# Gate rows built in pairs of tokens, and the later fetched rows' dot products ordered behind the first pass, in a one-core hybrid decoder step

## The chip, the cores and the metric

The kernel runs on one core of a Trainium2 chip. The metric is the device time of one execution in microseconds (us). The kernel before took 1742.75 us, the median of 3 runs (1738.49 to 1743.54).

## The reference, cut to what matters

One decoder layer over 512 prompt tokens and 32 sample tokens of width 1024: retention and a convolution share an input and an output projection, then a layer norm, and then PEER, a retrieval of experts by product keys. PEER is where the change lies. For each token, 8 heads pick 16 of 16384 experts each; the output is the sum over the 128 picked experts of a gate times a GELU of a dot product times a row:

```
idx = e1 * N_KEYS + e2                                   # 128 x 128 experts
gate = jax.nn.softmax(sv.astype(jnp.float32), axis=-1)
u = jnp.take(peer_u, idx, axis=0)
act = jax.nn.gelu(jnp.einsum('phkd,pd->phk', u, xb), approximate=False)
vv = jnp.take(peer_v, idx, axis=0)
return jnp.einsum('phk,phkd->pd', gate * act, vv)
```

A last layer norm and the new states follow.

## The kernel before, in words

The tokens are treated in two ways. For 288 of them the kernel fetches the expert rows: the first 128 prompt tokens (index tile `I`), the 32 samples (`Is`) and 128 more prompt tokens (`Ib`). For the last 256 prompt tokens (ND = 256) it computes all 16384 experts densely and multiplies by a gate that is zero for experts not picked.

**Fetched rows.** `gather` (L561 to L578) is a generator; one step of it is one slot k. GpSimd issues an indirect DMA (L566) that brings 128 rows of 2048 float32 values, u and v side by side, into a tile `g`; VectorE multiplies the u half by x1 and sums it (L569, the dot); ScalarE takes the GELU and multiplies by the gate (L571, L572); VectorE adds the weighted v half to `acc` (L577). The pool `gp` holds three such tiles; a fourth, in `gx` or `gx2`, is used where k % 4 == 3 and the generator has 128 slots. The samples have 32 slots of four heads' groups side by side, so they have the three tiles of `gp` alone. `fetched` (L931) finishes the first tokens, then runs the samples and then the `Ib` tokens, each with a layer norm and an output at its end (`finish`, L580).

**Dense tokens.** The 128 first-key blocks e are in four groups, `EG` = (32, 20, 44, 32), kept as `Gb`, `Gc`, `Ga`, `Gd`. `scores_of(e)` (L770) loads 512 KB of u and runs 8 float32 matmuls into `sp` [128, 256] (each is two instructions in the profile). `v_stage(e)` (L901) loads 512 KB of v and runs 4 matmuls of 512 columns into `pB`. The loads go through SP's queue and share a pool of four tiles.

**The gates.** `build` (L843) makes the gates of 8 tokens (TB = 8) at a time. ScalarE writes `A` (L850: 8 instructions of 128 columns; L852: one of 1024), which is 1 at each token's first key and 0 elsewhere. VectorE writes `M` (L854), which marks the second key, and `B` (L857), which holds M times three bfloat16 parts of the gate. The layout of `M` is [key, token], 8 tokens beside each other, and that of `B` [part, key, token]. TensorE then multiplies, for each token, `A` by the token's column of `B` for the three parts (L863): the moving operand `B[:, q, :, t - t1]` reads one bfloat16 of every eight, that is, it goes on by 16 bytes per column. `first_keys` (L876, here called the first pass) does it for the first 96 second keys, 4 tokens to a PSUM tile, and multiplies the PSUM tile into `Gb`, `Ga` and `Gc` (L887, L889 for blocks of `Gc` that are not ready); every 12 tokens it also computes the scores of one block of `Gc` (`s_stage`, L867 to L874). `last_keys` (L894) does the last 32 keys, 16 tokens to a PSUM tile, for `Gd`.

**The order.** The first pass is emitted first; then `run` (L952) interleaves `phases` (v stages of all blocks, `last_keys`, and the scores of `Gd`) with two steps of `fetched` to each step of `phases`. The Tile framework schedules the instructions of each engine in its own modelled order of time, so instructions that are emitted later may stand earlier on an engine; each engine runs its list in order. `behind(ins, other)` (L163) puts an instruction after another of the same engine in that list, without a semaphore. After the last v stage, `layer_norm` from `pB` and four output DMAs end the kernel (L953 to L958).

Of the kernel before, what the change touches and what calls it, by code (L numbers as in the profile page):

```python
# [10 lines left out]
BF = mybir.dt.bfloat16  # L11
# [3 lines left out]
OP = mybir.AluOpType  # L15
# [3 lines left out]
D = 1024  # L19
# [5 lines left out]
PH, NK, TK = 8, 128, 16  # L25
# [6 lines left out]
TB = 8  # L32
KX = 60
UV = 4
EG = (32, 20, 44, 32)
E0S = (0, 32, 52, 96)

# [54 lines left out]
def tile_step(ctx: ExitStack, tc: tile.TileContext, a, o):  # L92
    nc = tc.nc
    V, S, T, G = nc.vector, nc.scalar, nc.tensor, nc.gpsimd

    per = ctx.enter_context(tc.tile_pool(name="per", bufs=1))
# [15 lines left out]
    def mmps():  # L112
        turn[0] += 1
        return banks[turn[0] % len(banks)].tile([128, 512], F32, name="mm")
# [7 lines left out]
    def cc(n):  # L122
        part, c, w = COFF[n]
        return cst[part][:, c:c + w]
# [29 lines left out]
    def bc_row(name, src, n, pool=per, q=nc.scalar, after=None):  # L154
        t = pool.tile([128, n], F32, name=name)
        load = q.dma_start(t, bass.AP(tensor=src.tensor, offset=src.offset, ap=[[0, 128], [1, n]]))
        if after is not None:
            behind(load, after)
        return t
# [3 lines left out]
    def behind(ins, other):  # L163
        tc.add_manual_dep(ins.ins, other.ins.name, mybir.DependencyInfo(
            mybir.DependencyClass.NoSync, mybir.DependencyReason.DATA), reason="order")

    def small(name, shape, dt=F32, bufs=2):
        return wk.tile(shape, dt, name=name, bufs=bufs)

    iot = per.tile([128, NK, TB], BF, name="iot")  # L170
    G.iota(iot, pattern=[[1, NK], [0, TB]], base=0, channel_multiplier=0, allow_small_or_imprecise_dtypes=True)
    row = per.tile([128, NK], BF, name="row")
    G.iota(row, pattern=[[1, NK]], base=0, channel_multiplier=0, allow_small_or_imprecise_dtypes=True)
    mhalf = per.tile([128, 1], F32, name="mhalf")
# [25 lines left out]
    def rope(w, blk, xT, n, col0, outs):  # L200

        def turn_head(h):
            pm = mmps()
            for c0, c1, dst in outs:
                A = dst[:, h]
                T.matmul(pm[:, c0:c1], perm, A, start=True, stop=True)
                B = small("ropeB", [128, 416], bufs=1)[:, :c1 - c0]
                V.tensor_mul(B, pm[:, c0:c1], cc("sin")[:, col0 + c0:col0 + c1])
                V.tensor_mul(A, A, cc("cos")[:, col0 + c0:col0 + c1])
                V.tensor_add(A, A, B)  # L210

# [251 lines left out]
    def mix_mm(n, gT, y, c0, wo, xT=None):  # L463

        banks_ = [mmps(), mmps()]
        if xT is not None:
            for q in range(2):
                residual(banks_[q], xT, range(q * 4, q * 4 + 4), c0)
        for src, k0 in ((y, 4), (gT, 0)):
            for q in range(2):  # L470
                for s in range(2):
                    for k in range(4):
                        last = T.matmul(banks_[q][:n, s * 256:(s + 1) * 256], src[:, k, c0:c0 + n],
                                        wo[q * 2 + s][:, k0 + k, :], start=(xT is None and k0 == 4 and s == 0 and k == 0),
                                        stop=(k0 == 0 and s == 1 and k == 3), skip_group_check=True)
        return banks_, last
# [79 lines left out]
        V.reciprocal(sm[:n], sm[:n])  # L556
        V.tensor_mul(gate[:n, e0:e0 + nh], ex[:n], sm[:n].unsqueeze(2).to_broadcast([n, nh, TK]))

    gx2 = []

    def gather(x1, idx, gate, acc, slots):  # L561

        for k in slots:
            spare = gx if x1 is x1_0 and k < KX else (gx2[0] if gx2 and len(slots) == 128 else None)
            t = (spare if spare is not None and k % 4 == 3 else gp).tile([128, 2 * D], F32, name="g")
            G.indirect_dma_start(out=t, out_offset=None, in_=a["uv"],  # L566
                                 in_offset=bass.IndirectOffsetOnAxis(ap=idx[:, k:k + 1], axis=0))
            act = gw.tile([128, 2], F32, name="act")
            V.scalar_tensor_tensor(t[:, :D], t[:, :D], 1.0, x1, op0=OP.mult, op1=OP.mult, accum_out=act[:, 0:1])  # L569
            wgt = gw.tile([128, 1], F32, name="wgt")  # L570
            S.activation(act[:, 1:2], act[:, 0:1], AF.Gelu)  # L571
            S.activation(wgt, act[:, 1:2], AF.Copy, scale=gate[:, k:k + 1])  # L572
            v = t[:, D:]
            if k == slots[0]:
                S.activation(acc, v, AF.Copy, scale=wgt)
            else:
                V.scalar_tensor_tensor(acc, v, wgt, acc, op0=OP.mult, op1=OP.add)  # L577
            yield  # L578
# [33 lines left out]
    e2T = per.tile([128, ND], BF, name="e2T")  # L612
    gtT = per.tile([128, 3, ND], BF, name="gtT")
# [37 lines left out]
    pm, last = mix_mm(128, g0, y0, 0, wo)  # L651
# [90 lines left out]
    mix_b(NS + 2 * C, C)  # L742
    caches()
    gather0 = gather(x1_0, I0, g0_gates, acc0, range(PH * TK))
    for _ in range(KX):
        next(gather0)
# [3 lines left out]

    uvp = ctx.enter_context(tc.tile_pool(name="uvp", bufs=UV, reuse_waits="tile"))
    gap = ctx.enter_context(tc.tile_pool(name="gap", bufs=1, reuse_waits="tile"))
# [9 lines left out]
    ln2 = [bc_row("lng", a["ln2_g"], D), bc_row("lnb", a["ln2_b"], D)]  # L762
    GW = {2: gap.tile([128, EG[2], ND], F32, name="Ga")}

    def place(e):

        g = max(i for i in range(4) if E0S[i] <= e)
        return GW[g][:, e - E0S[g]]

    def scores_of(e):  # L770

        u = uvp.tile([128, D], F32, name="uv").rearrange("p (k e) -> p k e", k=8)
        nc.sync.dma_start(u, a["ut"][e])
        sp = pdn.tile([128, ND], F32, name="sp")
        for k in range(8):
            T.matmul(sp, u[:, k], x1T[:, k, NG2:], start=(k == 0), stop=(k == 7))  # L776
        return sp
# [19 lines left out]
    for g in range(2):  # L797
# [9 lines left out]
        p = mmps().rearrange("p (q t) -> p q t", q=4)  # L807
# [16 lines left out]
    gb = gbs.enter_context(tc.tile_pool(name="gb", bufs=1, side="right", reuse_waits="tile"))  # L824
    GW[0] = gb.tile([128, EG[0], ND], F32, name="Gb")
    for e in range(EG[0]):
        S.activation(place(e), scores_of(e), AF.Gelu)
# [10 lines left out]
    for b in range(2):  # L838
        for q in range(2):
            residual(pB[b][q], x1T, range(q * 4, q * 4 + 4), NG2 + b * 128)  # L840
    GW[1] = gc.tile([128, EG[1], ND], F32, name="Gc")

    def build(bt, e0, ne, nt):  # L843


        pt = None
        for t1 in range(0, ND, TB):
            off = bt.tile([128, TB, NK], BF, name="off", bufs=1)
            for t in range(TB):
                S.activation(off[:, t], row, AF.Abs, bias=e1T[:, t1 + t:t1 + t + 1])  # L850
            A = bt.tile([128, TB, NK], BF, name="A")
            S.activation(A, off, AF.Relu, bias=1.0, scale=-1.0)  # L852
            M = bt.tile([128, ne, TB], BF, name="M")
            V.tensor_tensor(M, iot[:, e0:e0 + ne],  # L854
                            e2T[:, t1:t1 + TB].unsqueeze(1).to_broadcast([128, ne, TB]), op=OP.is_equal)
            B = bt.tile([128, 3, ne, TB], BF, name="B")
            V.tensor_tensor(B, M.unsqueeze(1).to_broadcast([128, 3, ne, TB]),  # L857
                            gtT[:, :, t1:t1 + TB].unsqueeze(2).to_broadcast([128, 3, ne, TB]), op=OP.mult)
            for t in range(t1, t1 + TB):
                if t % nt == 0:  # L860
                    pt = pdn.tile([128, nt, ne], F32, name="mm")
                for q in range(3):
                    T.matmul(pt[:, t % nt], A[:, t - t1], B[:, q, :, t - t1], start=(q == 0), stop=(q == 2))  # L863
                if t % nt == nt - 1:
                    yield pt, slice(t - nt + 1, t + 1)

# [9 lines left out]
    def first_keys():  # L876

        with tc.tile_pool(name="bt", bufs=2, reuse_waits="tile") as bt:
            done = 0
            for pt, ts in build(bt, 0, E0S[3], 4):  # L880
                for g, e0, e1, ready in ((0, 0, EG[0], True), (2, 0, EG[2], True), (1, 0, done, True), (1, done, EG[1], False)):
                    if e0 == e1:
                        continue
                    to = GW[g][:, e0:e1, ts]
                    part = pt[:, :, E0S[g] + e0:E0S[g] + e1].rearrange("p t e -> p e t")
                    if ready:
                        V.tensor_mul(to, to, part)  # L887
                    else:
                        V.tensor_copy(to, part)  # L889
                if ts.stop % 12 == 0 and done < EG[1]:  # L890
                    s_stage(E0S[1] + done, ts.stop)
                    done += 1

    def last_keys():  # L894

# [35 lines left out]
    def fetched():  # L931
# [3 lines left out]
        for g, c0, dst in (("s", 0, o[1].rearrange("b i d -> (b i) d")), ("b", NS, o[0][0, 128:256])):  # L935
# [11 lines left out]
            finish(x1g, [ac[:, 0:512], ac[:, 512:]], w_, [(0, w_, dst)], t)  # L947
            yield

    first_keys()  # L950
    gx2.append(ctx.enter_context(tc.tile_pool(name="gx2", bufs=1, reuse_waits="tile")))
    run((phases(), 1), (fetched(), 2))  # L952
    for b in range(2):  # L953
        t = uvp.tile([128, D], F32, name="uv")
# [50 lines left out]
```

## Time and profile before

| what | value |
|---|---|
| median of 3 runs | 1742.75 us |
| the profiled execution | 1744.1 us, span 1742.3 us |
| PE busy | 1635.5 us, 94% |
| VectorE (DVE) busy | 1250.1 us, 72% |
| ScalarE (ACT) busy | 603.4 us, 35% |
| GpSimd (POOL) busy | 375.6 us, 22% |
| moved by DMA | 503.75 MB, mean 289 GB/s |
| mean granted TensorE clock | 0.943 |

The profile is of one execution on the hardware. The span is the time from its first to its last instruction; 1.8 us of the execution lie outside it. PE is the matmul engine and PEld its weight loads, which run beside the matmuls; since matmuls are pipelined, a busy PE isn't a PE at its peak. Waits are put down to what released them. The chain of waits follows the work back from the last instruction and tells at each step what that step waited for.

### The profile page before, as it was taken

How to read it: one execution, taken by the hardware profiler on the slowest of the kernel's cores; microseconds unless marked ns; L12 is line 12 of the kernel's file. 1: busy time of each engine (PE TensorE's matmuls, PEld its weight loads, DVE VectorE, ACT ScalarE, POOL GpSimd, SP SyncE). 2: the span in 40 equal slices, each digit the busy share in tenths (PEclk: the TensorE clock that was granted, in tenths of full speed). 3: DMA queues.
4: the chain of work that ended last, by engine and by line, in shares of the span. 5: the costliest groups of instructions: out<-in, count | busy, mean ns of one | idle time of the engine just before them, and what ended most of it. 6: DMA issues, size and time to landing. Idle time of an engine off the chain costs nothing.

```text
span 1742.3 us, 20660 instructions
## 1 busy us (share of the span) xinstructions
PE 1635.5 (94%) x7014; PEld 1111.1 (64%) x7014; DVE 1250.1 (72%) x3037; ACT 603.4 (35%) x1687; POOL 375.6 (22%) x335
## 2 busy tenths in 40 slices
PE   7899899969599889999999999999999999999997
PEld 6887566547465578887877666544557665553443
DVE  4949899898658989999566776776665777776201
ACT  1324441452212323334334555541688211111000
POOL 1002222345222222200210110232222422222000
PEclk9899999979799999999998887699999999999998
DMA  9469679978987689955965551499988999999642
GB/s 361 156 211 363 251 257 336 346 266 280 370 322 260 243 317 355 357 190 168 354 251 194 184 202 37 159 415 423 395 291 309 359 424 424 423 424 424 213 154 99
DMA packets 99542, 503.75 MB, mean 289 GB/s; under 512 B 10183, under 2 KB 21191, under 8 KB 56549
## 3 DMA queue, kind: packets, MB, share of 16 engines
q0 software_dynamic: 42240, 305.12, 45.8%
q1 hardware_dynamic: 50749, 189.96, 29.4%
q10 hardware_dynamic: 6448, 7.36, 1.3%
q8 instruction: 55, 0.90, 0.2%
q14 instruction: 50, 0.41, 0.1%
HBM read 497.03 MB, written 5.80 MB: 289 GB/s over the span
## 4 chain that ended last, share of the span: by engine, by line
PE 58%; DVE 21%; DMA 14%; issue 4%; POOL 2%; ACT 1%; SPq 0%; DVEq 0%; POOLq 0%; ACTq 0%
PE pB L907 22%; PE sp L776 15%; PE mm L863 9%; DMA g<-in_uv_dram,I 7%; PE mm L196 5%; DVE acc L577 4%; DVE g L569 4%; PE mm L306 2%; DMA uv<-in_ut_dram 2%; PE mm L261 2%; DMA g<-in_uv_dram,Ib 2%; DMA g<-in_w_in_dram 1%; POOL g L566 1%; DVE oh L546 1%; DMA out_dram<-keys 1%
## 5 line engine op out<-in xcount | busy, mean ns | idle before, releaser
L776 PE MATMUL sp<-x1T,uv 128*128 128x256 f32 x2048 | 485.5, 396 | 19.4 <-ACT Ga L822 7.2
L776 PEld LDWEIGHTS sp<-x1T,uv 128*128 128x128 f32 x2048 | 403.0, 200 | 101.9 <-issue 25.1
L577 DVE SCALAR_TENSOR_TENSOR acc<-g,wgt,acc 128x1024 f32<-128x1024 f32 x285 | 365.1, 1281 | 93.9 <-ACT wgt L572 92.7
L566 POOL DMA_INDIRECT g<-in_uv_dram,I x128 | 167.6, 1310 | 437.3 <-DVE acc L577 228.1
L569 DVE SCALAR_TENSOR_TENSOR g<-g,x1g 128x1024 f32<-128x1024 f32 x160 | 195.3, 1223 | 68.1 <-DMA g<-in_uv_dram,Ib 60.5
L566 POOL DMA_INDIRECT g<-in_uv_dram,Ib x128 | 143.6, 1122 | 406.1 <-DVE acc L577 360.3
L571 ACT ACTIVATE act<-act 128x1 f32<-128x1 f32 x288 | 57.4, 200 | 493.8 <-DVE g L569 493.4
L863 PE MATMUL mm<-B,A 128*128 128x96 bf16 (+1 forms) x1536 | 188.5, 294 | 5.1 <-DVE Gc L889 3.8
L569 DVE SCALAR_TENSOR_TENSOR g<-g,x 128x1024 f32<-128x1024 f32 x128 | 155.8, 1217 | 40.2 <-DMA g<-in_uv_dram,I 38.4
L196 PE MATMUL mm<-x1T,w 128*128 128x384 f32 (+1 forms) x512 | 179.5, 505 | 3.3 <-ACT score L522 2.6
L863 PEld LDWEIGHTS <-A 128*128 128x128 bf16 x1536 | 139.2, 117 | 65.5 <-issue 19.8
L907 PE MATMUL pB<-uv,Ga 128*128 128x512 f32 x352 | 162.3, 604 | 1.1 <-DMA uv<-in_uv_dram 0.8
L850 ACT ACTIVATE off<-row,e1T 128x128 bf16<-128x128 bf16 x512 | 157.8, 388 | 4.0 <-PE mm L863 3.0
L196 PEld LDWEIGHTS mm<-x1T,w 128*128 128x128 f32 x512 | 96.9, 192 | 76.0 <-issue 40.4
L907 PE MATMUL pB<-uv,Gb 128*128 128x512 f32 x256 | 119.9, 622 | 0.4 <-DVE Gb L887 0.4
L907 PEld LDWEIGHTS pB<-uv,Ga 128*128 128x128 f32 x352 | 63.8, 190 | 82.8 <-issue 62.6
L907 PE MATMUL pB<-uv,Gd 128*128 128x512 f32 x256 | 110.1, 593 | 0.1
L852 ACT ACTIVATE A<-off 128x1024 bf16<-128x1024 bf16 x64 | 67.4, 1054 | 97.7 <-PE mm L863 97.3
L907 PEld LDWEIGHTS pB<-uv,Gb 128*128 128x128 f32 x256 | 49.6, 200 | 61.7 <-issue 54.3
L857 DVE TENSOR_TENSOR B<-M,gtT 128x2304 bf16<-128x2304 bf16 (+1 forms) x64 | 60.8, 953 | 38.3 <-PE mm L863 38.3
L907 PEld LDWEIGHTS pB<-uv,Gd 128*128 128x128 f32 x256 | 48.6, 190 | 61.5 <-issue 60.4
L566 POOL DMA_INDIRECT g<-in_uv_dram,Is x32 | 36.0, 1126 | 210.8 <-DVE acc L577 115.5
(277 smaller groups left out, 1787.0 us busy)
## 6 DMA issues: line engine op xcount, KB each, us to landing
uv<-in_ut_dram SPq DMA_DIRECT2D x128, 512.0 KB
uv<-in_uv_dram SPq DMA_DIRECT2D x128, 512.0 KB
w<-in_w_in_dram SPq DMA_DIRECT2D x18, 1024.0 KB
w<-in_w_query_dram SPq DMA_DIRECT2D x16, 1024.0 KB
w<-in_w_out_dram SPq DMA_DIRECT2D x7, 1024.0 KB
g<-in_uv_dram,I POOLq DMA_INDIRECT x128, 7.9
keys<-in_state_retention_dram ACTq DMA_DIRECT2D x4, 512.0 KB
out_dram<-keys SPq DMA_DIRECT2D x4, 512.0 KB
```

Source lines behind the costliest of these rows:

```text
L196: T.matmul(p[:, :n], w[m // 2][:, k, (m % 2) * 128:(m % 2 + 1) * 128], xT[:, k, c0:c0 + n], start=(k == 0), stop=(k == 7))
L261: T.matmul(p[:, :L], dg[:, k % 4], u_p[:, m, p0 + k:p0 + k + L], start=(k == 0), stop=(k == CK - 1))
L566: G.indirect_dma_start(out=t, out_offset=None, in_=a["uv"], in_offset=bass.IndirectOffsetOnAxis(ap=idx[:, k:k + 1], axis=0))
L569: V.scalar_tensor_tensor(t[:, :D], t[:, :D], 1.0, x1, op0=OP.mult, op1=OP.mult, accum_out=act[:, 0:1])
L571: S.activation(act[:, 1:2], act[:, 0:1], AF.Gelu)
L577: V.scalar_tensor_tensor(acc, v, wgt, acc, op0=OP.mult, op1=OP.add)
L776: T.matmul(sp, u[:, k], x1T[:, k, NG2:], start=(k == 0), stop=(k == 7))
L850: S.activation(off[:, t], row, AF.Abs, bias=e1T[:, t1 + t:t1 + t + 1])
L852: S.activation(A, off, AF.Relu, bias=1.0, scale=-1.0)
L857: V.tensor_tensor(B, M.unsqueeze(1).to_broadcast([128, 3, ne, TB]), gtT[:, :, t1:t1 + TB].unsqueeze(2).to_broadcast([128, 3, ne, TB]), op= ...
L863: T.matmul(pt[:, t % nt], A[:, t - t1], B[:, q, :, t - t1], start=(q == 0), stop=(q == 2))
L907: T.matmul(pB[b][q], W[:, b * 128:(b + 1) * 128], vt[:, q * 512:(q + 1) * 512], start=False, stop=(e == NK - 1), skip_group_check=True)
```

## The change

`M` and `B` hold the tokens in pairs: `M` is [pair, key, 2] and `B` is [part, pair, key, 2], so the moving operand of L863 goes on by 4 bytes per column where it went on by 16. `B` is written by three VectorE instructions, one for each part, where one wrote it; `iot` shrinks from 8 copies of each key to 2. Besides, `first_keys` hands back its last multiplication as `fence`, and in the generators that are emitted after it the dots of the samples from slot 12 (FREE) on, and all dots of the `Ib` tokens, are put behind that multiplication on VectorE.

```diff
+FREE = 12
-    iot = per.tile([128, NK, TB], BF, name="iot")
-    G.iota(iot, pattern=[[1, NK], [0, TB]], base=0, channel_multiplier=0, allow_small_or_imprecise_dtypes=True)
+    iot = per.tile([128, NK, 2], BF, name="iot")
+    G.iota(iot, pattern=[[1, NK], [0, 2]], base=0, channel_multiplier=0, allow_small_or_imprecise_dtypes=True)
...
-    gx2 = []
+    gx2, fence = [], []
...
-            V.scalar_tensor_tensor(t[:, :D], t[:, :D], 1.0, x1, op0=OP.mult, op1=OP.mult, accum_out=act[:, 0:1])
+            dot = V.scalar_tensor_tensor(t[:, :D], t[:, :D], 1.0, x1, op0=OP.mult, op1=OP.mult, accum_out=act[:, 0:1])
+            if fence and (len(slots) == 128 or k >= FREE):
+                behind(dot, fence[0])
...
+    def pairs_of(x, t1):
+        return x[:, t1:t1 + TB].rearrange("p (a b) -> p a b", b=2).unsqueeze(2)
...
-            M = bt.tile([128, ne, TB], BF, name="M")
-            V.tensor_tensor(M, iot[:, e0:e0 + ne],
-                            e2T[:, t1:t1 + TB].unsqueeze(1).to_broadcast([128, ne, TB]), op=OP.is_equal)
-            B = bt.tile([128, 3, ne, TB], BF, name="B")
-            V.tensor_tensor(B, M.unsqueeze(1).to_broadcast([128, 3, ne, TB]),
-                            gtT[:, :, t1:t1 + TB].unsqueeze(2).to_broadcast([128, 3, ne, TB]), op=OP.mult)
+            M = bt.tile([128, TB // 2, ne, 2], BF, name="M")
+            V.tensor_tensor(M, iot[:, e0:e0 + ne].unsqueeze(1).to_broadcast([128, TB // 2, ne, 2]),
+                            pairs_of(e2T, t1).to_broadcast([128, TB // 2, ne, 2]), op=OP.is_equal)
+            B = bt.tile([128, 3, TB // 2, ne, 2], BF, name="B")
+            for q in range(3):
+                V.tensor_tensor(B[:, q], M, pairs_of(gtT[:, q], t1).to_broadcast([128, TB // 2, ne, 2]), op=OP.mult)
...
-                    T.matmul(pt[:, t % nt], A[:, t - t1], B[:, q, :, t - t1], start=(q == 0), stop=(q == 2))
+                    T.matmul(pt[:, t % nt], A[:, t - t1], B[:, q, (t - t1) // 2, :, t % 2], start=(q == 0), stop=(q == 2))
...
-                        V.tensor_mul(to, to, part)
+                        last = V.tensor_mul(to, to, part)
...
+        return last
...
-    first_keys()
+    fence.append(first_keys())
```

## The prediction

> **What bounds the kernel now.** I read the page's busy times and its chain of waits first, then windows of the two parts that the change touches, then pieces of the chain inside them.
>
> ```profile
> PE 1635.5 (94%) x7014; PEld 1111.1 (64%) x7014; DVE 1250.1 (72%) x3037; ACT 603.4 (35%) x1687; POOL 375.6 (22%) x335
> PE 58%; DVE 21%; DMA 14%; issue 4%; POOL 2%; ACT 1%; SPq 0%; DVEq 0%; POOLq 0%; ACTq 0%
> ```
>
> TensorE leads, but the shares are averages. The first pass runs from 880 us (its first multiplication into `Gb`) to 1116 us; from there the second part runs to the last v stage at 1731 us. The windows view gives each engine's busy time, the granted clock and the DMA rate:
>
> ```profile
> core 0: us, PE busy (x) PEld busy (x) DVE busy (x) ACT busy (x) POOL busy (x), PEclk, DMA share, GB/s
> 880.00:1116.00 236.00, 228.12 (x1078) 166.20 (x1076) 160.37 (x403) 123.43 (x356) 28.75 (x25) 0.79 0.45 159
> 1116.00:1731.00 615.00, 608.81 (x2288) 329.83 (x2288) 354.26 (x487) 182.83 (x576) 134.29 (x126) 1.00 0.87 343
> 1731.00:1742.30 11.30, 0.00 (x0) 0.00 (x0) 5.53 (x12) 2.89 (x4) 0.79 (x2) 0.59 0.24 93
> ```
>
> Both parts are TensorE's, but the first leaves two thirds of VectorE, half of ScalarE and half of the DMA rate, while the second has DMA at 0.87. Pieces of the chain (start, us, what) give the prices:
>
> ```profile
> 1003.73 6.50 PE sp L776 x16
> 1098.90 16.81 PE mm L863 x96
> 1241.63 1.44 PE mm L863 x24
> 1373.01 3.45 PE sp L776 x16
> 1376.46 3.43 PE pB L907 x8
> 1571.38 7.37 PE pB L907 x16
> ```
>
> A gate matmul of 96 columns takes 16.81 / 96 = 175 ns, one of 32 columns 60 ns: 1.8 ns per column in both, so a gate matmul's pace goes with its columns, and loading `A` is hidden within 60 ns. A score matmul with its operand side by side takes 3.45 / 16 / 256 = 0.84 ns per column. What sets the gate matmuls apart is the 16-byte step. The first row, a score stage of 6.50 us, also shows a low clock in this pass. The pass needs 768 gate matmuls (134 us) and 20 score stages (69 us) of TensorE, plus what the low clock adds: that is the 228.
>
> **The change part by part.**
>
> *Gate matmuls of the first pass.* 24 are done before 880; 744 remain. Their new price isn't in the trace. Lower bound, an estimate: half of the score matmul's 0.84 ns per column, 40 ns. Upper bound: nothing gained, 175 ns; short of that, the score matmul's pace, which also goes on by 4 bytes a column, 81 ns. I take 60, the fastest gate matmul that the trace has, with the same weight load. TensorE then needs 744 x 60 ns = 45, 69 for the score stages and 7 for two early v stages (2 x 3.43): 121 us. Every 10 ns is 7 us.
>
> [...]
>
> *VectorE in the pass.* Its pieces in one stretch, and the shapes:
>
> ```profile
> 1094.57 0.20 DVE Gb L887
> 1094.77 0.25 DVE Ga L887
> 1095.01 0.13 DVE Gc L887
> 1095.15 0.08 DVE Gc L889
> 1095.23 1.26 DVE B L857
> 1096.49 0.47 DVE M L854
> ```
>
> ```profile
> L857 DVE TENSOR_TENSOR B<-M,gtT 128x2304 bf16<-128x2304 bf16 x32 | 43.1, 1349 | 1.4 <-PE mm L863 1.4
> L546 DVE TENSOR_TENSOR oh<-row,pf 128x800 bf16<-128x800 bf16 x34 | 33.5, 984 | 0.1
> L854 DVE TENSOR_TENSOR M<-iot,e2T 128x768 bf16<-128x768 bf16 x32 | 17.5, 552 | 0.0
> ```
>
> Four tokens cost 0.66 us of multiplications, eight cost 2 x 0.66 + 1.26 + 0.47 = 3.05. After, `B` is three instructions of `M`'s size, 3 x 0.47 = 1.41 if rows of two run as fast as rows of eight: 3.2 per eight tokens, about 30 x 3.2 = 96 us, with 20 multiplications of `s_stage` (0.3 each) 102. The other end is L546's pace, a bfloat16 operation at 1.23 ns per element against `M`'s 0.72: 0.4 us more in each of four instructions, 1.6 per eight tokens. I take the fast end, since operands and result are still neighbours in pairs, and keep the slow end as a rival. The smaller `iot` lies at the start of GpSimd's list, where nothing waits for it: nothing.
>
> *ScalarE in the pass* is untouched:
>
> ```profile
> 1092.52 1.06 ACT L852 ACTIVATE A<-off 128x1024 bf16<-128x1024 bf16 x1
> 1098.99 2.44 ACT L850 ACTIVATE off<-row,e1T 128x128 bf16<-128x128 bf16 x8
> ```
>
> 3.5 us per eight tokens, 105 us for 30, and some 10 for `s_stage`: 115.
>
> *The pass.* TensorE 121, ScalarE 115, VectorE 102: nearly level, so order matters. In the built instruction order the last 180 gate matmuls follow the last score stage of the pass, and there ScalarE's 7.5 x 3.5 = 26 us lead. Ahead of them TensorE has 121 - 11 = 110. Together 136; with 7 us (an estimate) for ramps and waits 143, so the pass ends at 880 + 143 = 1023 where it ended at 1116: 93 us earlier. The score stages' low clock would cost 20 x (3.45 / 0.79 - 3.45) = 18 more if it stayed; I expect most of it to go, since the matmuls that hold PE without streaming go.
>
> *The fetched rows.* In the built order, 35 dots of samples and `Ib` stand ahead of the pass's last multiplication before, 12 after. So 125 rows' dots lie behind it before and 148 after: 23 more rows, with their transfers of 1.05 MB (128 x 2048 x 4 bytes), fall into the second part. That is what relieves VectorE in the pass (23 x 2.5 us); GpSimd's issues of these rows wait for tiles, with nothing else behind them on its queue but the samples' layer norm. Transfers in the second part, by windows of the issuing line:
>
> ```profile
> 1160.00:1230.00 70.00, 20.30 (x19) 1.00 1.01 423
> 1237.00:1390.00 153.00, 43.05 (x32) 1.00 0.88 326
> 1404.00:1600.00 196.00, 49.26 (x53) 1.00 1.02 424
> ```
>
> At 424 GB/s DMA is full and a row takes 196 / 53 = 3.7 us; beside the last keys it is 153 / 32 = 4.8, since VectorE works in order and its `B` waits for the matmuls of two builds before. The end of the rows and of the kernel before:
>
> ```profile
> 1622.00 1.28 DVE L577 SCALAR_TENSOR_TENSOR acc<-g,wgt,acc 128x1024 f32<-128x1024 f32 x1 [0.60 <-ACT wgt L572]
> 1631.04 0.34 SPq L587 DMA_DIRECT2D out_dram<-yt  x1
> 1728.04 0.70 DVE L445 BATCH_NORM_STATS2 lst<-pB 128x6 f32<-128x512 f32 x1 [97.03 <-PE pB L907]
> ```
>
> The rows took 1623 - 1116 = 507 us and their layer norm 8; the rows' 100 us of lead over TensorE is what the deferral spends. After: 507 + 23 x 3.7 to 4.4 (the samples have three tiles, not four) = 592 to 608, and 10 to 15 for the samples' layer norm, which no longer lies in the pass (the 9 us from 1622.00 to 1631.04, with three more additions): about 612, with the last layer norm 620 behind the pass's end.
>
> TensorE in the second part took 615. It runs a v stage in 3.69 us (7.37 / 2) under full DMA, against 3.43; full DMA covered 19 + 58 stages (two windows at 3.7 each) and will cover some 50 more, 50 x 0.25 = 12. Against that, 32-column gate matmuls may drop from 60 to 40 ns, 768 x 20 ns = 15 at most; I take none to 10. So 620. Bytes alone: 148 rows and 158 loads of 0.52 MB are 238 MB, at 424 GB/s 561 us: no bound of its own.
>
> *Sum.* 1023 + 620 + 11.3 (last layer norm and output, the third window) = 1654 of span; 1.8 us outside it (1744.1 against 1742.3) make 1656, and the median of the runs lies 1.35 below the profiled one: **1655 us**, 88 faster. VectorE's and ScalarE's new work in the last keys (0.3 us per build) hides beside v stages of 3.43.
>
> **The rivals.**
>
> *The rows become the tail* (18%). For: the lead of 100 us is used up, and both ends stand within 10 us of each other. At 4.4 us per row, between full DMA and the last keys' stretch, 148 rows take 651, and with 12 + 11 the part lasts 674: 1023 + 674 = 1697, so about 1698.
>
> *Rows of two halve VectorE's rate* (8%). 30 x 1.6 = 48 us more in the pass: VectorE at 150 leads all of it, end at 880 + 150 + 20 for waits on TensorE, thus 1050 or so: 1682. Against it: operands and result keep neighbours.
>
> *No gain on the gate matmuls* (6%). TensorE keeps 204 in the pass, which loses only VectorE's share of the chain (about 8 us in its last 40), and the second part gains its 5 to 30: 1740 to 1765, say 1745. Against it: the pace per column.
>
> *Slower: the rows keep the last keys' pace throughout* (5%). Place: VectorE's list in the second part. Price: 148 x 0.1 = 15 us for each 0.1 us of a row. To lose the 93 us, rows and ends must take 708, so (708 - 23) / 148 = 4.6 us per row; at the 4.8 of the second window it would be 710 + 23, and the kernel 1023 + 733 = 1756. Against it: there are 24 builds behind which this holds, in the order before and after alike, and some 21 rows among them; the rest met full DMA.
>
> **How the numbers follow.** Forecast 63%, with its own range 1625 to 1685 (matmul at 40 or 81 ns: -8 or +15; clock +18; second part -20 to +15). The 80% range takes in the slow VectorE and most of the tail: 1618 to 1705. Faster by over 0.3%, which is about what a measurement of this kernel can tell from no change: 63 + 18 + 8 and a sixth of "no gain", 90%; same 3%; slower 7% (the last rival and a third of "no gain").
>
> **What would show it.** Two rows of the waits in the pass (in all, times, longest):
>
> ```profile
> ACT A L852 <- PE mm L863: 95.1, 27, 7.5
> DVE Gb L887 <- PE mm L863: 69.5, 41, 4.3
> ```
>
> Both engines stand waiting for the gate matmuls now; after, these rows should shrink to a few tens. Further: L863 at 96 columns near 60 ns, 24 in about 1.4 us; the last multiplication of the pass near 1023 us; three `B` of about 550 ns each; 148 dots behind the pass; the last accumulation within 20 us of the last v stage. Wrong would be: 96-column matmuls above 100 ns, `B` parts near 900 ns, or a last accumulation far behind the v stages.

## The result, and the profile after

The changed kernel takes 1611.09 us (median of 4 runs, 1605.78 to 1614.02), the kernel before beside it on the same chip 1740.62 us (1735.44 to 1743.54): a ratio of 0.9255, 95% interval 0.922 to 0.929. The forecast was 1655, the range 1618 to 1705. The direction was right; the gain is half as large again as forecast (130 us, not 88).

The profiled execution took 1605.8 us with a span of 1604.0. First its page: busy time of each engine, and the chain of waits by engine.

```profile
PE 1492.6 (93%) x7014; PEld 1008.7 (63%) x7014; DVE 1259.6 (79%) x3165; ACT 603.9 (38%) x1687; POOL 364.6 (23%) x335
DMA 18%; ACT 6%; issue 4%; DVE 3%; POOL 1%; DVEq 0%; POOLq 0%; ACTq 0%
```

143 us of TensorE's busy time are gone. The chain, which named PE for 58% before, now has no PE in it: it begins at 1100 us and runs through ScalarE's gate rows and the fetched rows, whose transfers alone are 18% of the span. Yet PE is still busy for 93%. Two ends lie close together, and the chain follows only the one that came last. The windows view of the same three stretches as in the prediction (pass, second part, tail):

```profile
core 0: us, PE busy (x) PEld busy (x) DVE busy (x) ACT busy (x) POOL busy (x), PEclk, DMA share, GB/s
866.00:996.50 130.50, 116.54 (x1078) 99.57 (x1077) 102.78 (x385) 108.14 (x302) 0.98 (x2) 0.93 0.30 104
996.50:1587.00 590.50, 583.95 (x2284) 300.58 (x2284) 416.04 (x617) 197.94 (x629) 155.01 (x147) 1.00 0.98 398
1587.00:1604.00 17.00, 2.11 (x5) 0.57 (x3) 11.21 (x22) 4.13 (x5) 3.54 (x6) 0.68 0.24 93
```

Two boundaries of this view lie a little off those of the other kernels' views: the pass's last multiplication ends at 996.1 us, and TensorE's last matmul at 1589.1. Cut there, the pass is 130.4 us, the second part 593.0 (TensorE busy for 586.45 of it) and the tail 14.9; these numbers are used from here on. The pass fell from 236 us to 130.4 and its granted clock rose from 0.79 to 0.93; the three engines are nearly level in it. The second part fell from 615 to 593, though 23 more rows lie in it, with TensorE busy for 99% of it and DMA for 98%. The tail grew from 11.3 to 14.9.

Where TensorE's time went, in its timeline (start, us, instructions). A group's printed time runs past the start of the next group (in the third row to 868.58 + 1.20 = 869.78 us, 0.16 us behind the fourth row's start; called the drain here), so the pace is read from one group's start to the next one's start. First two rows of the kernel before, then the kernel after:

```profile
882.81 4.28 PE L863 MATMUL mm<-B,A 128*128 128x96 bf16 x24
886.91 5.12 PE L776 MATMUL sp<-x1T,uv 128*128 128x256 f32 x16
```

```profile
868.58 1.20 PE L870 MATMUL mm<-B,A 128*128 128x96 bf16 x24
869.62 3.68 PE L779 MATMUL sp<-x1T,uv 128*128 128x256 f32 x16
...
967.27 0.66 PE L779 MATMUL sp<-x1T,uv 128*128 128x256 f32 x2
...
980.47 2.08 PE L870 MATMUL mm<-B,A 128*128 128x96 bf16 x24 [2.21 <-DVE Gc L896]
...
1206.34 1.35 PE L870 MATMUL mm<-B,A 128*128 128x32 bf16 x48
1207.54 3.70 PE L779 MATMUL sp<-x1T,uv 128*128 128x256 f32 x16
```

24 matmuls of 96 columns take 869.62 - 868.58 = 1.04 us, 43 ns each (forecast 60; before 175 by the prediction's row with the drain in it, 171 from start to start). Behind waits such as that at 980.47 the same 24 take 2.08 us; the granted clock from 968 us to the pass's end is 0.69. 48 of 32 columns take 1.20 us, 25 ns each (before 60, forecast 60, or 47 with the 10 us that the forecast allowed). A score stage in the pass takes 3.70 us on average (319 matmuls in 73.77 us), where it took 4.66 before (318 in 92.56 us); the prediction's row of 6.50 was a slow one. The groups of VectorE and TensorE, with their mean ns:

```profile
L865 DVE TENSOR_TENSOR B<-M,gtT 128x768 bf16<-128x768 bf16 x96 | 47.8, 552 | 0.0
L870 PE MATMUL mm<-B,A 128*128 128x96 bf16 x768 | 44.4, 215 | 12.3 <-DVE Gc L896 11.3 <-DVE Gc L894 0.9
L870 PE MATMUL mm<-B,A 128*128 128x32 bf16 x768 | 24.2, 176 | 0.0
```

`B` in pairs costs 552 ns for each part, exactly what `M` in eights cost. The waits in the pass (in all, times, longest):

```profile
DVE Gb L894 <- PE mm L870: 27.5, 22, 2.1
ACT A L859 <- PE mm L870: 16.9, 18, 1.9
...
PE mm L870 <- DVE Gc L896: 11.3, 10, 2.2
```

The two waits that the prediction named, 69.5 and 95.1 us, are 27.5 and 16.9, and one in the other direction has grown: TensorE waits 11.3 us, 3.8 before, for PSUM tiles that VectorE has not yet read. The end of the kernel: the dots behind the pass, the last accumulation, and the last weight load of the last v stage:

```profile
L570 DVE SCALAR_TENSOR_TENSOR g<-g,x1g x148: 1204/1226/1227, 996.3 to 1582.4; 128x1024 f32<-128x1024 f32 x148
```

```profile
1584.19 1.28 DVE L580 SCALAR_TENSOR_TENSOR acc<-g,wgt,acc 128x1024 f32<-128x1024 f32 x1 [0.60 <-ACT wgt L575]
...
1588.09 0.19 PEld L915 LDWEIGHTS pB<-uv,Gd 128*128 128x128 f32 x1 [0.24 <-issue]
1588.16 1.24 DVE L446 BATCH_NORM_STATS2 lst<-pB 128x6 f32<-128x512 f32 x2
```

148 dots as forecast, and both ends within 4 us of each other. That they meet goes with the longer tail: the layer norm of the last rows and that of `pB` now share VectorE, ScalarE and GpSimd (VectorE is busy for 9.1 us of the tail, 5.5 before), and where the rows end earlier (e1, e6, e7 below) the tail is 11.3 to 11.6 us.

### The profile page after: what moved, and what is told of

Read it like the earlier page. It is cut to its first block, busy times and chain, and to the rows that moved or that the text cites. A ratio compares the mean times of both kernels' runs of the same rounds, so it can differ in the third digit from the quotient of the medians.

```text
span 1604.0 us, 20824 instructions
## 1 busy us (share of the span) xinstructions
PE 1492.6 (93%) x7014; PEld 1008.7 (63%) x7014; DVE 1259.6 (79%) x3165; ACT 603.9 (38%) x1687; POOL 364.6 (23%) x335
## 5 line engine op out<-in xcount | busy, mean ns | idle before, releaser
L779 PE MATMUL sp<-x1T,uv 128*128 128x256 f32 x2048 | 465.5, 383 | 17.7 <-ACT Ga L825 8.1
L779 PEld LDWEIGHTS sp<-x1T,uv 128*128 128x128 f32 x2048 | 384.7, 191 | 90.7 <-issue 22.4
L567 POOL DMA_INDIRECT g<-in_uv_dram,I x128 | 161.5, 1261 | 433.0 <-DVE acc L580 230.3
L567 POOL DMA_INDIRECT g<-in_uv_dram,Ib x128 | 135.8, 1061 | 485.4 <-DVE acc L580 313.8
L915 PE MATMUL pB<-uv,Gd 128*128 128x512 f32 x256 | 117.2, 601 | 2.0 <-DMA uv<-in_uv_dram 0.8
L915 PE MATMUL pB<-uv,Gb 128*128 128x512 f32 x256 | 115.0, 603 | 2.1 <-DMA uv<-in_uv_dram 1.7
L870 PEld LDWEIGHTS <-A 128*128 128x128 bf16 x1536 | 64.5, 99 | 37.0 <-issue 29.0
L870 PE MATMUL mm<-B,A 128*128 128x96 bf16 (+1 forms) x1536 | 68.6, 196 | 12.3 <-DVE Gc L896 11.3
L865 DVE TENSOR_TENSOR B<-M,gtT 128x768 bf16<-128x768 bf16 (+1 forms) x192 | 69.7, 419 | 6.1 <-PE mm L870 6.0
L915 PE MATMUL pB<-uv,Gc 128*128 128x512 f32 x160 | 72.3, 599 | 0.0
```

The costliest lines, as they stand in the source:

```text
L567: G.indirect_dma_start(out=t, out_offset=None, in_=a["uv"], in_offset=bass.IndirectOffsetOnAxis(ap=idx[:, k:k + 1], axis=0))
L865: V.tensor_tensor(B[:, q], M, pairs_of(gtT[:, q], t1).to_broadcast([128, TB // 2, ne, 2]), op=OP.mult)
L870: T.matmul(pt[:, t % nt], A[:, t - t1], B[:, q, (t - t1) // 2, :, t % 2], start=(q == 0), stop=(q == 2))
L915: T.matmul(pB[b][q], W[:, b * 128:(b + 1) * 128], vt[:, q * 512:(q + 1) * 512], start=False, stop=(e == NK - 1), skip_group_check=True)
```

## The experiments

Theory A, after the two traces: the 16-byte step alone set the gate matmuls' pace; in pairs they reach a floor, which is worth 100 us in the pass and 27 us in the last keys, and the fence is there so that VectorE does not take TensorE's place in the pass. Against it stood: B, that the pace goes with the step and has not reached a floor; C, that the deferral of the rows is most of the gain; D, that the rows' transfers, not the strided matmuls, lowered the clock; E, that the rows' end hides TensorE's gain in the second part. The times are medians. The ratios are against the kernel before on the same chip, whose median moves between 1738.94 and 1745.19 us from chip to chip, so that a difference of two times can be some 5 us off what the ratios give.

| kernel | step, fence | us | ratio, 95% interval |
|---|---|---|---|
| after | 4 bytes, slot 12 | 1611.09 | 0.9255 (0.922 to 0.929) |
| e1 | 4 bytes, none | 1651.73 | 0.9458 (0.9408 to 0.9509) |
| e2 | 16 bytes, slot 12 | 1742.09 | 0.9981 (0.9952 to 1.0011) |
| e3 | 8 bytes, slot 12 | 1643.15 | 0.9407 (0.9364 to 0.9450) |
| e4 | 4 bytes, in the last keys 16, slot 12 | 1634.97 | 0.9365 (0.9321 to 0.9409) |
| e5 | 2 bytes, slot 12 | 1638.14 | 0.9420 (0.9385 to 0.9454) |
| e6 | 4 bytes, slot 16 | 1609.39 | 0.9254 (0.9229 to 0.9278) |
| e7 | 4 bytes, slot 20 | 1613.38 | 0.9277 (0.9248 to 0.9306) |

**e1, the pairs without the fence.**

```diff
...
-            if fence and (len(slots) == 128 or k >= FREE):
-                behind(dot, fence[0])
...
```

> Pairs kept, the fence left out (so some 35 fetched rows' dots stand ahead of the pass's last multiplication again, not 12). Theory A (the 16-byte step sets the gate matmuls' pace; the fence only keeps VectorE out of TensorE's way): L870 at 96 columns stays at 43 ns, TensorE is busy some 117 us in the pass, but VectorE has 103 us plus 23 rows x 2.5 us = 160 us there and ends it: pass of 165 to 175 us in place of 130, the second part shorter by 5 to 20 us since 23 rows fewer fall into it; 1620 to 1640 us. Rival C (the deferral is most of the gain, the pairs little): 96-column matmuls near 43 ns do not matter, and the time lies at 1690 to 1740 us. If the start of the pass lies near 866 us as in the kernel after, the pairs or the schedule made it earlier, not the fence.

Measured: 1651.73 us. Windows of its pass, second part and tail:

```profile
873.70:1039.70 166.00, 129.08 (x1079) 107.96 (x1078) 161.77 (x465) 122.76 (x355) 34.81 (x26) 0.84 0.65 232
1039.70:1637.00 597.30, 586.09 (x2288) 303.27 (x2288) 357.45 (x549) 182.24 (x579) 143.88 (x126) 0.99 0.89 353
1637.00:1648.30 11.30, 0.00 (x0) 0.00 (x0) 5.54 (x12) 2.89 (x4) 0.79 (x2) 0.72 0.24 93
```

One row of the waits in its pass:

```profile
PE mm L868 <- DVE Gc L894: 30.9, 16, 3.9
```

Theory A's pass of 165 to 175 us came, at its lower end: VectorE is busy for 161.77 of 166 us, and TensorE waits for it, 30.9 us where the kernel after has 11.3 (the same code stands at L896 there). The second part was to become 5 to 20 us shorter and did not: 597.3 us with 125 rows, 593.0 with 148. So the 23 rows that the fence moves cost the second part nothing that shows, and the time came out 12 us above the expected range. The rows end 107 us ahead of the last v stage's end here; TensorE, busy for 586.09 us, alone sets this second part.

**e2, the fence without the pairs.** The build is that of the kernel before.

```diff
...
+            if fence and (len(slots) == 128 or k >= FREE):
+                behind(dot, fence[0])
...
```

> Tokens in eights as before, the fence added. Theory A: L870 at 96 columns stays at 175 ns, TensorE keeps some 205 to 220 us of work in the pass, which loses only VectorE's part of the waits: pass of 215 to 230 us; 148 rows behind it at 3.7 to 4.4 us take 550 to 640 us, against 1116 - 880 of before, so the end of the rows is late: 1725 to 1765 us, no gain to speak of. Rival C: the deferral frees VectorE and with it the pass, 1640 to 1700 us. Rival D (the low granted clock comes from DMA traffic in the pass and not from the strided matmuls): the clock in the pass rises from 0.79 to over 0.9 here, since the rows no longer come in the pass.

Measured: 1742.09 us, no change that this can tell. Its pass and second part:

```profile
871.20:1099.00 227.80, 227.42 (x1079) 168.10 (x1078) 100.44 (x324) 108.76 (x301) 0.00 (x0) 0.79 0.17 57
1099.00:1723.00 624.00, 617.15 (x2288) 328.80 (x2288) 413.16 (x556) 200.21 (x629) 159.89 (x147) 0.99 0.94 376
```

VectorE is relieved by 60 us of the pass (100.44, not 160.37), and TensorE, busy for 227.4 of 227.8 us, takes no notice: the pass gives 8 us, the second part takes 9. C falls. D falls too: the transfers in the pass are down from 159 to 57 GB/s, and the clock stays at 0.79. It is the matmuls with the 16-byte step that go with the low clock.

With e1 the two parts of the change can be added up, and they don't add: the fence is worth nothing that shows in eights and 41 us in pairs (1651.73 against 1611.09; 35 by the ratios).

**e3, tokens in fours: a step of 8 bytes.**

```diff
-            M = bt.tile([128, TB // 2, ne, 2], BF, name="M")
+            M = bt.tile([128, TB // 4, ne, 4], BF, name="M")
...
-                    T.matmul(pt[:, t % nt], A[:, t - t1], B[:, q, (t - t1) // 2, :, t % 2], start=(q == 0), stop=(q == 2))
+                    T.matmul(pt[:, t % nt], A[:, t - t1], B[:, q, (t - t1) // 4, :, t % 4], start=(q == 0), stop=(q == 2))
```

> [...] Rival B (the pace goes with the step): 96 columns at 80 to 90 ns, which is 744 x 40 = 30 us more in the pass, 32 columns at about 30 ns; 1635 to 1650 us.

Measured: 1643.15 us. Its timeline in the pass and in the last keys:

```profile
981.93 2.25 PE L870 MATMUL mm<-B,A 128*128 128x96 bf16 x24
984.00 3.66 PE L779 MATMUL sp<-x1T,uv 128*128 128x256 f32 x16
...
1144.51 1.70 PE L870 MATMUL mm<-B,A 128*128 128x32 bf16 x48
1146.04 7.11 PE L915 MATMUL pB<-uv,Gc 128*128 128x512 f32 x16
```

24 in 2.07 us: 86 ns per 96 columns, 0.90 ns per column, half of 1.8 and twice 0.45. 48 of 32 columns take 1.53 us, 32 ns each. So rival B holds for the step from 16 to 4 bytes: at 96 columns every halving of the step halved the time of a column. Fours do not cost what pairs cost: the trace shows 86 ns, not 43.

**e5, one token after the other: a step of 2 bytes.** Now `M` and `B` have the keys of one token side by side, and VectorE reads `gtT` and `e2T` with one element over a whole row.

```diff
-            M = bt.tile([128, TB // 2, ne, 2], BF, name="M")
+            M = bt.tile([128, TB, ne], BF, name="M")
...
-                    T.matmul(pt[:, t % nt], A[:, t - t1], B[:, q, (t - t1) // 2, :, t % 2], start=(q == 0), stop=(q == 2))
+                    T.matmul(pt[:, t % nt], A[:, t - t1], B[:, q, t - t1], start=(q == 0), stop=(q == 2))
```

> One token after the other, its 96 (or 32) columns side by side: the moving operand steps 2 bytes, and VectorE's M and B read e2T and gtT with the same element over a whole row, not in pairs. Theory B (pace goes with the step: 1.82, 0.90 and 0.45 ns per column were measured at 16, 8 and 4 bytes) without a floor: 96 columns at 20 to 25 ns; with a floor at the weight load's pace (32 columns took 25 ns at 4 bytes, not 14): 25 to 43 ns; 43 exactly if 4 bytes is the floor already. For the time VectorE decides: if such rows run at L546's pace (1.23 ns per element in place of 0.72), M and three B take 4 x 0.94 = 3.8 us in place of 2.2 per eight tokens, 30 x 1.6 = 48 us more, VectorE has some 150 us in the pass and ends it: 1640 to 1665 us. If they keep 0.72 ns per element: 1603 to 1618 us, as with pairs.

Measured: 1638.14 us, 2 us below the range that was given for slow VectorE rows. First the group of `B`, then the pass in the windows view, then TensorE's timeline in it:

```profile
L865 DVE TENSOR_TENSOR B<-M,gtT 128x768 bf16<-128x768 bf16 x96 | 86.7, 963 | 0.0
```

```profile
871.10:1026.00 154.90, 120.11 (x1073) 102.29 (x1072) 146.84 (x384) 108.20 (x301) 0.94 (x1) 0.87 0.25 85
```

```profile
956.42 1.12 PE L870 MATMUL mm<-B,A 128*128 128x96 bf16 x12 [2.88 <-DVE Gc L896]
957.34 5.76 PE L779 MATMUL sp<-x1T,uv 128*128 128x256 f32 x16
962.94 1.18 PE L870 MATMUL mm<-B,A 128*128 128x96 bf16 x24
963.96 3.69 PE L779 MATMUL sp<-x1T,uv 128*128 128x256 f32 x16
```

24 matmuls in 1.02 us, 42.5 ns: no gain over pairs (43 ns), so 4 bytes is the floor already. VectorE pays for the layout: 963 ns where pairs cost 552, 146.84 us busy in the pass instead of 102.78, and the pass is 24 us longer (154.9). VectorE's pace is that of L546, as expected: 963 / 768 = 1.25 ns per element. Pairs are therefore the one layout among the four that is slow on neither engine: a gate matmul of 96 columns takes 171 ns in eights and 86 in fours against 43, and a part of `B` takes 963 ns in singles against 552. In fours (e3) it takes 559; in eights one instruction wrote all three parts in 1349. So a part of `B` was slow only where `gtT` gives one element for a whole row.

**e4, the last keys in eights again,** the first pass as in the kernel after (`build8` is the build of the kernel before).

```diff
...
-            for pt, ts in build(bt, E0S[3], EG[3], 16):
+            for pt, ts in build8(bt, E0S[3], EG[3], 16):
```

> The first pass in pairs with the fence; the last keys' build in eights as before (step of 16 bytes, 32 columns at 60 ns in place of 25). Theory A (TensorE ends the second part, and the 32-column matmuls are the term that the prediction sized wrong): 768 x 35 ns = 27 us later, 1632 to 1642 us. Rival E (the rows' transfers end the second part, and TensorE's time there has cover): +0 to 10 us, 1605 to 1621 us.

Measured: 1634.97 us, 24 us above the kernel after (19 by the ratios). Its pass and second part:

```profile
861.30:987.00 125.70, 115.01 (x1079) 98.74 (x1078) 103.92 (x386) 107.90 (x303) 0.94 (x1) 0.95 0.33 114
987.00:1610.00 623.00, 616.95 (x2288) 328.03 (x2288) 413.55 (x556) 200.04 (x629) 156.56 (x147) 0.99 0.94 377
```

The second part is 30 us longer than in the kernel after, and so is TensorE's busy time (616.95 us, not 586.45). E falls: although the chain of the kernel after runs through the rows, most of a longer TensorE is paid for. The rows here end at 1607, 620 us behind the pass, and not at 589 as in the kernel after, with the same 148 of them: VectorE takes them in one list with the last keys' `B`, which waits 49.3 us for the matmuls here and 6.0 in the kernel after, and the loads of v share DMA with them (0.94 busy here). Two ends that meet this closely are no two independent bounds.

**e6 and e7, the fence from slot 16 and from slot 20.**

```diff
-FREE = 12
+FREE = 16
```

> Pairs, and the fence from slot 16 on, so 4 more fetched rows' dots and additions (4 x 2.5 = 10 us of VectorE) stay in the pass, where VectorE is idle for 27 of 130 us, and the rows behind it are 144, not 148 (4 x 3.7 = 15 us less). Theory: pass 130 to 134 us, the rows end 10 to 15 us ahead of the last v stage, the tail falls from 17 to some 12 us: 1598 to 1609 us, -2 to -8 against the kernel after. Rival: the four rows' dots wait for their transfers on VectorE, in front of the multiplications that TensorE needs: pass up to 140, 1609 to 1618 us.

> The fence from slot 20 on: 8 more rows in the pass, 20 us of VectorE, which then has 123 us there, more than TensorE's 117. Theory: pass 138 to 145 us, the second part 3 to 6 us shorter than the kernel after's (less DMA beside the last v stages, shorter tail): 1604 to 1615 us. Rival (VectorE has still room): 1596 to 1604 us.

Measured: 1609.39 and 1613.38 us. e6's pass, second part and tail, then e7's:

```profile
874.60:1001.30 126.70, 115.20 (x1079) 98.79 (x1078) 111.83 (x396) 108.57 (x311) 5.75 (x5) 0.94 0.41 142
1001.30:1596.00 594.70, 587.36 (x2288) 301.14 (x2288) 411.82 (x616) 197.78 (x622) 161.06 (x147) 1.00 0.96 389
1596.00:1607.60 11.60, 0.00 (x0) 0.00 (x0) 5.83 (x12) 2.89 (x4) 0.89 (x3) 0.73 0.23 90
```

```profile
873.50:1006.30 132.80, 117.21 (x1079) 100.23 (x1078) 121.07 (x408) 110.52 (x319) 10.18 (x9) 0.93 0.47 164
1006.30:1601.00 594.70, 586.42 (x2288) 302.05 (x2288) 402.58 (x604) 196.59 (x614) 153.35 (x143) 1.00 0.95 382
1601.00:1612.40 11.40, 0.00 (x0) 0.00 (x0) 5.58 (x12) 2.90 (x4) 0.79 (x2) 0.71 0.24 92
```

The tail falls to 11.6 us as expected, since the rows end 21 us ahead of the last v stage's end in e6; the second part, 594.7, is no shorter than in the kernel after (593.0, and 594.2 in e8). Counted from its start of the pass, e6's profiled execution takes 733.0 us, the kernel after's two 738.3 and 740.7, but the ratios are the same (0.9254 and 0.9255), so the gain of 2 to 8 us that was expected isn't shown. In e7 the pass is 132.8 us where 138 to 145 were expected: VectorE still had room. Neither is told apart from the kernel after (the intervals lie over each other); between 12 and 20 the place of the fence hardly matters, while no fence costs some 40 us.

**e8 and e9, both kernels profiled once more,** unchanged, to see what the start of the pass does. In the kernel after it lay 14 us earlier than in the kernel before.

> The kernel after, unchanged, profiled once more. Its pass began at 865.7 us in the first profile, at 874.6 and 873.5 in the kernels with the fence at 16 and 20, whose orders agree with it ahead of the pass. If that difference is from run to run, the pass begins anywhere in 861 to 878 here, and lasts 128 to 133 us; if it is the built order, within 3 us of 866.

> The kernel before, unchanged, profiled once more. If the start of the pass (880.0 us in its first profile, 861 to 874 in the five changed kernels) varies from run to run, it lies anywhere in 860 to 885 here; if it hangs on the built order of the instructions, it lies within 3 us of 880.

Measured: 1616.48 and 1743.85 us. The multiplications into `Gb` (min, median and max ns, first and last start), first of e8, then of e9:

```profile
L894 DVE TENSOR_TENSOR Gb<-Gb,mm x64: 265/277/290, 873.8 to 1005.0; 128x128 f32<-128x128 f32 x64
```

```profile
L887 DVE TENSOR_TENSOR Gb<-Gb,mm x64: 267/288/289, 875.9 to 1112.2; 128x128 f32<-128x128 f32 x64
```

The same kernel starts its pass at 865.7 us in one execution and at 873.8 in another, the kernel before at 880.0 and 875.9. So the same kernel's start moves by up to 8 us from one execution to another. The later two ran on different chips and the chips of the first two aren't on record, so run and chip aren't told apart in this. The profiled execution of the kernel after (1605.8) lies 5 us below its median. What is left of the 14, 2 us between the later two profiles, lies within this scatter; whether the changed order ahead of the pass has a part in it stays open.

## Why the prediction was right or wrong, point by point

The sum was 1023 + 620 + 11.3 = 1654 of span; measured are 996.1 + 593.0 + 14.9 = 1604. The 50 us are: the pass began 14 us earlier, was 130.4 us long and not 143 (-12.6), the second part 593.0 and not 620 (-27), the tail 14.9 and not 11.3 (+3.6). This is the fastest of the four executions; in e8's, 10.5 us longer, 8.1 are the start of the pass, and the pass and the second part have 1.2 each.

- **What bounds the kernel: right.** The step set the gate matmuls' pace in both parts: at 16, 8 and 4 bytes 171, 86 and 43 ns for 96 columns, and 60, 32 and 25 ns for 32.
- **Gate matmuls at 60 ns: the step that failed.** The prediction took "60, the fastest gate matmul that the trace has, with the same weight load" for 96 columns and kept about 60 for 32 columns ("I take none to 10" us). Measured are 43 and 25 ns. In the pass 540 gate matmuls lie ahead of the end of the last score stage, where TensorE leads: 540 x 17 ns = 9 of the 12.6 us by which the pass was short. The other 204 go at ScalarE's pace, so that their price hardly counts. In the second part the gate matmuls are busy for 24.2 us and not 51.1: 27 us, of which the forecast had at most 10, so 17 to 27 were missing. e4, which gives the second term back alone, is 24 us slower. With these two prices in its own sum the forecast would have been 1655 - 9 - 17 to 27 = 1619 to 1629 (an estimate); the early start of the pass and the overpriced full DMA (below) are about what is left. The row that was taken for a floor was a 16-byte row itself: the prediction says that both shapes take 1.8 ns per column, and a price that still goes with the columns is not a floor. The bound that it gave for 96 columns, 40 ns, was the right end; for 32 columns its end of 40 ns was too high, with no row behind it.
- **The rival of no gain on the gate matmuls: rightly priced low.** It would have left the matmul of 96 columns at 175 ns; it takes 43.
- **VectorE in the pass: right.** 102 us forecast, 102.78 measured, three `B` of 552 ns. The rival "rows of two halve VectorE's rate" did not come, but its price was right: e5, in which the rate does fall, is 27 us above the kernel after, as the rival was to be above the forecast (1682 against 1655).
- **The order of the pass: right.** The last score stage in the pass ends at 968 us, and the gate matmuls behind it (204, not 180) take to 996, 28 us where 26 were forecast under ScalarE's lead; ScalarE is busy for 26.0 of these 28.1 us.
- **The clock: right.** The score stages' low clock went (4.66 to 3.70 us on average), and e2 shows that it goes with the matmuls' step and not with the rows: 0.79 in the pass at 57 GB/s as at 159, where the kernel after has 0.93. What joins the step and the clock is not shown.
- **The fetched rows: right in number and order, too long in time.** 148 dots lie behind the pass, and the rows end 4 us ahead of the last v stage's end, within the 10 us that were forecast. But they take 1585.5 - 996.3 = 589 us, the samples' layer norm included, where about 612 were forecast: 4.0 us per row in all. That the rows would become the tail came only in the 3.6 us of the longer tail; that they would keep the last keys' pace did not happen.
- **Full DMA beside the v stages: overpriced.** In the second part the matmuls of the v stages are busy for 454.6 us before (DMA busy for 0.87 of the part) and 458.3 after (0.98), those of the score stages for 117.6 and 117.5. So full DMA cost some 4 us and not 12, and with the 27 us of the gate matmuls that is the whole of the second part's change (614.5 to 593.0, within 2 us). e1, e6 and e7, with 125 to 144 rows in place of 148, have 456.1 to 457.8 us of v stages.
- **The tail: missed by 3.6 us, the other way.** The two layer norms were added one after the other in thought; the case that both ends meet and share three engines was not priced. e6 and e7, whose rows end earlier, have 11.6 and 11.4.
- **The range** ended at 1618. The forecast's own fast end, 1625, had the gate matmul at 40 ns for -8 us, where "Every 10 ns is 7 us" gives about -15, and -20 for the second part, which gave -27; for the 7 us below it there is no working. The start of the pass, which moves by 8 us between executions, was in none of its terms.
- **Readings of the trace that don't hold.** The first pass does not leave two thirds of VectorE but a third: 160 of 236 us were busy. The 768 gate matmuls that the prediction adds up for it are 744 between 880 and 1116 us, and two v stages (10.25 us) belong to its 228. And 196 us at 3.7 are 53 stages, not 58. None of these moved the forecast by more than a few us.

## What to carry to other kernels

Before a row of the trace is taken as the floor of an operation, see whether its time still goes with its size: here 96 and 32 columns both took 1.8 ns per column, and their prices fell to 43 and 25 ns. Choose a layout that two engines read by pricing it on both: here TensorE took 43 ns a matmul at a step of 4 bytes and 86 at 8, VectorE 552 ns a part of `B` in pairs and 963 in singles, and only one layout of four is fast on both. When one bound is lifted, ask what stands right below it: the fence is worth nothing while TensorE leads the pass and some 40 us once it doesn't.

## What the runs showed of the hardware that was not expected

- In the gate matmuls of 96 columns (bfloat16) the time of a column went with the step of the moving operand: 1.8 ns at 16 bytes, 0.90 at 8, 0.45 at 4, and 0.44 at 2, where it no longer fell. A gate matmul with its weight load did not go below 25 ns (32 columns at 4 and at 2 bytes; 32 ns at 8, 60 at 16).
- Some stops of TensorE were followed by slow matmuls. In e5 the score stage that follows a wait of 2.88 us and 12 gate matmuls takes 5.76 us, the next one 3.69. In the kernel after, 24 gate matmuls behind a wait of 2.21 us take 2.08 us in place of 1.20 (both with the drain). But a wait of 3.73 us in e5 (at 994 us) was followed by 24 in 1.25 us, where 24 without a wait take 1.18. The clock granted in the pass was lower where TensorE idled more, at steps of 4 and 2 bytes: 0.93 in the kernel after (14 of 130 us idle), 0.87 in e5 (35 of 155), 0.84 in e1 (37 of 166). And a PE that was busy all the time had a low clock too: 0.79 in e2 (227.4 of 227.8 us busy), with matmuls of the 16-byte step in the pass.
- The same program's first 870 us differed by 8 us from one execution to another (865.7 and 873.8 us in the kernel after), half a per cent of the whole.
